# Attention branch product of an encoder layer in seven half-size products instead of eight, with its weights and y kept raw in SBUF

## The chip, the cores and the metric

One core of a Trainium2 chip runs the whole program. A core has five engines with a queue each: TensorE (PE, matrix products out of SBUF into PSUM; PEld is its loading of weights), VectorE (DVE), ScalarE (ACT), GpSimd (POOL) and SyncE (SP, here only a queue that issues DMAs). An engine works its queue in order and waits on semaphores for the others. The metric is device microseconds for one execution, the median of several runs.

## The reference

The program is one layer of an encoder, 1024 positions of 1024 channels in float32:

```python
h = rmsnorm(x, g_mix)
z = h @ w_in                                   # pooling channels | q | k | v
y_pool = pool_mixer(u_pool, w_pool_grp, pool_scale)          # S x 512
y_attn = diff_attention(q, k, v, g_q, g_k, lam, g_sub, ...)  # S x 1024, 8 heads
gates = sigmoid(h @ w_gate + b_gate)                         # S x 2048
merged = (gates[..., :D] * (y_pool @ w_branch_pool)
          + gates[..., D:] * (y_attn @ w_branch_attn))
x = x + merged @ w_out
h2 = rmsnorm(x, g_ffn)
x = x + square(relu(h2 @ w_up)) @ w_down
```

The change lies in `merged`: the product with `w_branch_attn` (1024 x 1024 by 1024 x 1024, transposed: channels in partitions, positions along the row) and the gating of both branches.

## The kernel before

**Precision.** Each product is made of three: an operand is split into a high part, rounded to fp32r by a cast on ACT (`split`, L120), and a low part, operand minus high part, on DVE or POOL (L121). `mm3` (L126 to L128) adds hi x hi, hi x lo and lo x hi in one PSUM bank. So each operand tile costs one ACT cast and one subtraction, and each 128 x 128 x 512 block three matmuls.

**Stages.** Attention with the products for the gates and the pooling mixer as filler ends at about 701 us of the span. `g_dram` then holds the gates before their sigmoid, `y_dram` and `r_dram` the attention output and its row factors, `p_dram` the pooling branch. After it come three stages and then the MLP (up from 926 us, down to the end):

- *bp*, 701 to 745 us: `branch_pool` makes 16 tiles of 128 channels by 512 positions, 12 matmuls each (four blocks of depth 128), out of `wbp` and `ypT`. ACT copies each tile from PSUM to `mp`. Beside it `y_scaled` loads y and multiplies it with its factors (`ry`, L215), and `split_halves` makes `yT` of it, high and low part for all 8 blocks of depth; both stay in SBUF for the next stage.
- *ba*, 745 to 832 us: for each block d of 128 channels `load_cols` loads and splits one column block of the weights (`wba`, low part on POOL), `gate` loads the gates and takes their sigmoid, DVE multiplies `mp` with its gate (L837). Then two tiles of 24 matmuls; each is multiplied with its gate out of PSUM (`mg`, L844, DVE), POOL adds `mp` (L845), and `split` makes `mT`, the operand of the next stage (cast on ACT, low part on DVE).
- *op*, 832 to 926 us: `out_proj` multiplies `mT` with w_out (`wo`, low part on POOL), adds x and norms the rows.

**Order of the work.** The kernel is written as a program in one order; a scheduler then sets the order of each engine's queue by its own estimate of when operands and buffers are there, and puts in the semaphores. Buffers rotate in pools: a load or a write into a slot waits until the last reader of what lay there has finished. PSUM has eight banks, and `bank` takes them in turn.

Of the kernel before, what the change touches and what calls it, by code (L numbers as in the profile page):

```python
# [32 lines left out]
N_U, N_W, N_RAW, N_V = 11, 8, 2, 6  # L33
# [2 lines left out]
N_Z, N_S, N_T, N_F = 2, 2, 2, 1  # L36
N_YU = 5
N_QKVW = 8 * H
ROOMS = "WWFFWWWFFWWW"
N_AHEAD_Y = 4  # L40


START = "x0 g n0 w0 w1 w2u w3u x1 s0p s1 x2 s2p s3 x3"
# [14 lines left out]
def encoder_kernel(  # L58
# [32 lines left out]
    hp1 = mix.enter_context(tc.tile_pool(name="hp1", bufs=8))  # L91
# [9 lines left out]
    hcount = [0]  # L101

    def htile(shape, dt, name, th):

        if th == 0:
            hcount[0] += 1
        return (hp1 if th else hp0[(hcount[0] - 1) // 4 % 2]).tile(shape, dt, tag="H", name=name)
# [10 lines left out]
    def split(hi, lo, src, lo_eng=None):  # L118

        nc.scalar.copy(hi, src)  # L120
        (lo_eng or nc.vector).tensor_tensor(lo, src, f(hi), op=ALU.subtract)  # L121

    def mm3(ps, lhs_hi, lhs_lo, rhs_hi, rhs_lo, first, last, more=False):

        kw = {"skip_group_check": True} if more else {}
        nc.tensor.matmul(ps, lhs_hi, rhs_hi, start=first, stop=False, **kw)  # L126
        nc.tensor.matmul(ps, lhs_hi, rhs_lo, start=False, stop=False, **kw)  # L127
        nc.tensor.matmul(ps, lhs_lo, rhs_hi, start=False, stop=last, **kw)  # L128

    wcount = [0]  # L130

    def wt(shape, name):

        wcount[0] += 1
        if wcount[0] > N_QKVW and ROOMS[(wcount[0] - N_QKVW - 1) // 2] == "F":
            return fw_tile(shape, name)
# [14 lines left out]
    def load_cols(src, c0, name, nk=NK):

        rw = raw([P, nk, P], f"r{name}")
        nc.sync.dma_start(rw, src[0 : nk * P, c0 : c0 + P].rearrange("(kk p) c -> p kk c", p=P))
        ws = []
        for j in range(0, nk, 4):
            w = wt([P, 2, 4, P], f"w{name}_{j}")
            split(w[:, 0], w[:, 1], rw[:, j : j + 4, :], nc.gpsimd)
            ws.append(w)
        return ws  # L160

    def load_cols2(src, c0, name):

        rw = raw([P, 4, 2 * P], f"r{name}")
        nc.sync.dma_start(rw, src[0 : 4 * P, c0 : c0 + 2 * P].rearrange("(kk p) c -> p kk c", p=P))
        ws = []
        for j in range(2):
            w = wt([P, 2, 4, P], f"w{name}_{j}")
# [49 lines left out]
    def gate(gts, c):  # L218
        for gt, c0, c1 in gts:
            nc.sync.dma_start(gt, g_dram[c * P : (c + 1) * P, c0:c1])  # L220
            nc.scalar.activation(gt, gt, AF.Sigmoid, bias=zero)

    def whole(g):
        return [(g, 0, S)], [g[:, 0:512], g[:, 512:S]]
# [12 lines left out]

# [565 lines left out]
    nbank.append(0)  # L803


    def row_factors(d):
        if d < N_AHEAD_Y or d == 5:
            return [fu_tile(f"rb{d}")]
        if d == 4:
            return [ut([P, S], F32, f"rb{d}")]  # L810
        return [tmp(f"rb{d}_{i}") for i in range(2)]

    ws_bp = {0: load_cols2(w_branch_pool, 0, "bp0")}
    ys = {d: y_scaled(d, row_factors(d)) for d in range(N_AHEAD_Y)}
    ypT = [load_split(p_dram, g * P, f"ypT{g}", ypt_tile) for g in range(4)]
    mp, yT, ws_ba = [], [], {}

    for d in range(NK):
        if d % 2 == 0 and d + 2 < NK:
            ws_bp[d + 2] = load_cols2(w_branch_pool, (d + 2) * P, f"bp{d + 2}")  # L820
        elif d > NK - 4:
            j = len(ws_ba)
            ws_ba[j] = load_cols(w_branch_attn, j * P, f"ba{j}")
        branch_pool(d, ws_bp[d - d % 2][d % 2], bank)
        yT.append(split_halves(ys.pop(d), f"yT{d}", yt_tile(d)))
        if d + N_AHEAD_Y < NK:
            ys[d + N_AHEAD_Y] = y_scaled(d + N_AHEAD_Y, row_factors(d + N_AHEAD_Y))
    mT = {}
    for d in range(NK):
        if d + 3 < NK:  # L830
            ws_ba[d + 3] = load_cols(w_branch_attn, (d + 3) * P, f"ba{d + 3}")
        ws = ws_ba.pop(d)
        gp = [tmp(f"gp{d}_{th}") for th in range(2)]
        gate([(gp[0], 0, 512), (gp[1], 512, S)], d)
        for th in range(2):
            mh = mp[d][:, th * 512 : (th + 1) * 512]
            nc.vector.tensor_tensor(mh, mh, gp[th], op=ALU.mult)  # L837
        ga = fu_tile(f"ga{d}") if d % 2 else ut([P, S], F32, f"ga{d}")
        gate(whole(ga)[0], NK + d)
        for th in range(2):  # L840
            hs = slice(th * 512, (th + 1) * 512)
            ps = proj_T(bank(f"ba{d}_{th}"), ws, lambda k, th: pair(yT[k][th]), th)
            mg = tmp(f"mg{d}_{th}")
            nc.vector.tensor_tensor(mg, ps, ga[:, hs], op=ALU.mult)  # L844
            nc.gpsimd.tensor_tensor(mg, mg, mp[d][:, hs], op=ALU.add)  # L845
            t = htile([P, 2, 512], F32R, f"mT{d}_{th}", th)
            split(t[:, 0, :], t[:, 1, :], mg)
            mT[d, th] = t
# [365 lines left out]
    b11 = {}  # L1218
# [117 lines left out]
```

## Time and profile before

| what | value |
|---|---|
| median of 3 runs | 1549.02 us (1548.29 to 1549.4) |
| the profiled execution | 1548.34 us, its span 1546.6 us |
| granted TensorE clock | 1.0 |
| TensorE busy | 1526.0 us, 99% of the span |
| stage bp | 701.3 to 745 us |
| stage ba | 745 to 832 us |
| stage op | 832 to 926 us |

All durations are from the one profiled execution. A row of a group reads: line, engine, operation, output <- inputs by their names in the program, shape, count | busy time, mean ns of one | idle time of the engine ahead of them and who ended it. A row of the timeline reads: start us, length us, engine, line, operation, and in brackets how long the engine sat idle before it. In the table by stretches of time each engine has its busy time and, in parentheses, its count of instructions; then the granted clock and the DMA engines' share. Since matmuls overlap in the pipeline, the length of one (390 ns for 512 columns) is not the interval between two.

### The profile page before, as it was taken

To read this page: it belongs to the slowest core of one execution; us is meant where nothing else is said; L and a number is where in the kernel's file an instruction comes from. 1 tells how busy PE (TensorE), PEld (TensorE's weight loads), DVE (VectorE), ACT (ScalarE), POOL (GpSimd) and SP (SyncE) were. 2 spreads that over 40 slices of the span, in tenths; PEclk is the share of its full clock that TensorE was granted. 3 is DMA by queue.
4 is the path that set the end of the run, shared out by engine and by line. 5 is a ranking of instruction groups with operands and counts; after the bars stand their busy time and mean duration, and the time that the engine had idled before them with its cause. 6 is when DMAs were issued, how large, how long until landed. Compare 5 with 4: busy or idle time off the path is not lost.

```text
span 1546.6 us, 22053 instructions
## 1 busy us (share of the span) xinstructions
PE 1526.0 (99%) x7649; PEld 1320.4 (85%) x7649; DVE 1012.4 (65%) x2268; ACT 816.5 (53%) x1808; POOL 350.9 (23%) x448
## 2 busy tenths in 40 slices
PE   7999999999999999999999999999999999999999
PEld 6899999999998989888888887888888788888887
DVE  7777777777878787865322448766666668556672
ACT  6656555666666565566432546565555634333331
POOL 6433334243525262315443400000000000000000
PEclk9999999999999999999999999999999999999999
DMA  7111212020202031547426534555432789537650
GB/s 230 49 54 48 64 39 73 20 79 32 81 28 84 28 96 42 177 132 250 139 93 205 177 105 124 180 172 176 137 136 109 259 312 389 196 123 256 225 192 28
DMA packets 166681, 206.41 MB, mean 133 GB/s; under 512 B 10069, under 2 KB 102954, under 8 KB 166570
## 3 DMA queue, kind: packets, MB, share of 16 engines
q1 hardware_dynamic: 149162, 177.71, 34.8%
q10 hardware_dynamic: 17408, 27.30, 4.7%
q8 instruction: 60, 0.98, 0.3%
q14 instruction: 51, 0.42, 0.1%
HBM read 150.42 MB, written 54.56 MB: 133 GB/s over the span
## 4 chain that ended last, share of the span: by engine, by line
PE 91%; DVE 3%; issue 2%; ACT 1%; DMA 1%; POOL 1%; SPq 1%; POOLq 0%; DVEq 0%; ACTq 0%
PE z L126 5%; PE z L128 5%; PE z L127 5%; PE Da L126 4%; PE Da L127 4%; PE Da L128 4%; PE g L126 3%; PE g L127 3%; PE g L128 3%; PE Db L126 3%; PE Db L127 3%; PE Db L128 3%; PE X L126 2%; PE X L128 2%; PE X L127 2%; PE sc L512 2%
## 5 line engine op out<-in xcount | busy, mean ns | idle before, releaser
L126 PE MATMUL z<-wqkv,hT 128*128 128x384 f32 x512 | 174.5, 341 | 0.4 <-DVE qn L453 0.3
L128 PE MATMUL z<-wqkv,hT 128*128 128x384 f32 x512 | 174.1, 340 | 0.0
L127 PE MATMUL z<-wqkv,hT 128*128 128x384 f32 x512 | 173.8, 339 | 0.0
L522 ACT ACTIVATE s<-s,nm 128x256 f32<-128x256 f32 (+7 forms) x128 | 99.6, 778 | 45.8 <-DVE nm L514 42.7
L260 POOL TENSOR_TENSOR ms<-ms,mhalf 128x4 f32<-128x4 f32 x64 | 66.5, 1039 | 158.0 <-DVE ms L259 136.7
L126 PE MATMUL g<-hT,fwgate 128*128 128x512 f32 x256 | 101.0, 395 | 0.1
L127 PE MATMUL g<-hT,fwgate 128*128 128x512 f32 x256 | 101.0, 395 | 0.0
L128 PE MATMUL g<-hT,fwgate 128*128 128x512 f32 x256 | 101.0, 395 | 0.0
L126 PEld LDWEIGHTS z<-wqkv,hT 128*128 128x128 f32 x512 | 96.8, 189 | 3.9 <-DVE qn L453 1.0
L127 PEld LDWEIGHTS z<-wqkv,hT 128*128 128x128 f32 x512 | 96.6, 189 | 3.0
L128 PEld LDWEIGHTS z<-wqkv,hT 128*128 128x128 f32 x512 | 96.6, 189 | 2.2 <-DVE hT L121 0.5
L514 DVE CUSTOM_DVE_ANT_0 s<-sc,dist 128x512 f32<-128x512 f32 (+3 forms) x128 | 74.7, 586 | 19.7 <-PE sc L512 18.2
L121 POOL TENSOR_TENSOR wqkv<-rqkv,wqkv 128x384 fp32r<-128x384 f32 x60 | 64.0, 1085 | 19.2 <-ACT wqkv L120 15.5
L121 DVE TENSOR_TENSOR AS<-s,AS 128x512 fp32r<-128x512 f32 x64 | 43.9, 688 | 35.8 <-ACT AS L120 35.6
L511 PE MATMUL sc<-K,Q 128*128 128x512 f32 (+2 forms) x192 | 66.6, 353 | 0.1
L512 PE MATMUL sc<-K,Q 128*128 128x512 f32 (+2 forms) x192 | 66.5, 354 | 0.0
L459 POOL TENSOR_TENSOR qn<-qn,ggh 128x128 f32<-128x128 f32 x64 | 32.3, 505 | 138.7 <-DVE qn L453 127.7
L485 ACT CAST Q<-tk 64x128 fp32r<-64x128 f32 x128 | 33.2, 259 | 57.8 <-DVE Q L484 56.0
L482 ACT CAST Q<-tk 64x128 fp32r<-64x128 f32 x128 | 33.0, 258 | 53.7 <-DVE K L481 52.3
L121 POOL TENSOR_TENSOR fwgate<-frgate,fwgate 128x512 fp32r<-128x512 f32 x32 | 44.5, 1394 | 51.9 <-ACT fwgate L120 51.8
L128 PEld LDWEIGHTS g<-hT,fwgate 128*128 128x128 f32 x256 | 48.1, 188 | 8.6
L126 PEld LDWEIGHTS g<-hT,fwgate 128*128 128x128 f32 x256 | 48.2, 188 | 7.3 <-ACT go L757 0.4
(430 smaller groups left out, 4640.7 us busy)
## 6 DMA issues: line engine op xcount, KB each, us to landing
wd<-in_w_down_dram SPq DMA_DIRECT2D x56, 512.0 KB, 5.3
wu<-in_w_up_dram SPq DMA_DIRECT2D x32, 512.0 KB, 4.5
udS<-us SPq DMA_DIRECT2D x64, 256.0 KB, 2.4
ur<-udS SPq DMA_DIRECT2D x32, 512.0 KB, 3.3
rqkv<-in_w_in_dram SPq DMA_DIRECT2D x64, 192.0 KB, 2.7
ud<-u ACTq DMA_DIRECT2D x48, 256.0 KB, 2.1
ur<-ud SPq DMA_DIRECT2D x24, 512.0 KB, 4.7
frgate<-in_w_gate_dram SPq DMA_DIRECT2D x32, 256.0 KB, 2.6
```

What stands on the lines that cost most here:

```text
L121: (lo_eng or nc.vector).tensor_tensor(lo, src, f(hi), op=ALU.subtract)
L126: nc.tensor.matmul(ps, lhs_hi, rhs_hi, start=first, stop=False, **kw)
L127: nc.tensor.matmul(ps, lhs_hi, rhs_lo, start=False, stop=False, **kw)
L128: nc.tensor.matmul(ps, lhs_lo, rhs_hi, start=False, stop=last, **kw)
L260: nc.gpsimd.tensor_tensor(dst, dst, mhalf[:, :n], op=ALU.pow)
L459: nc.gpsimd.tensor_tensor(qn[:, 2:4, :], qn[:, 2:4, :], ggh.unsqueeze(1).broadcast_to([P, 2, HD]), op=ALU.mult)
L482: nc.scalar.copy(q_hi, q)
L485: nc.scalar.copy(Q[other, m, 1, :], q)
L511: nc.tensor.matmul(dst, Q[:, i, 0, :], rhs, start=True, stop=False)
L512: nc.tensor.matmul(dst, Q[:, i, 1, :], rhs, start=False, stop=True)
L514: nc.vector.tensor_tensor_reduce(out=s[i][:, c : c + w], in0=sc[:, 0:w], in1=dist[:, o0 + c : o0 + c + w], scale=2.0 ** -(h + 1), scalar=B ...
L522: nc.scalar.activation(s[i][:, 0:n], s[i][:, 0:n], AF.Exp, bias=last, scale=-1.0, accum_out=Z[:, i, t : t + 1])
```

## The change

The product with `w_branch_attn` is cut into quarters of 512 x 512 x 512: weights a11, a12, a21, a22 and y b11, b12, b21, b22. Instead of eight products of quarters it makes seven, over sums and differences of quarters, in the order 1, 2, 6, 7, 5, 4, 3 (Winograd's form of Strassen's product). Four products of the seven go on adding to a bank that holds another's result, and copies of three partial results are kept in SBUF ("slabs" x1, U2, z7). Each product has four steps of depth 128, and a step is 12 matmuls, over four banks.

- Raw weights come in contiguous rows (`load_wr`, 8 x 512 KB) and stay in SBUF as `wr`, as y does in `ry`; the sums overwrite them in place on DVE (`first_sums`, `second_sums`, `third_sums`: 32 operations of 128 x 512).
- Three steps ahead of TensorE, `prepare` splits the two operands of a step: `wa` (cast ACT, low part POOL) into one of four "fw" slots and `yb` (cast ACT, low part DVE) into one of four "B" slots. `wba` and `yT` go, with their splits: 16 of each before, 28 of each now.
- `after` takes a product's banks: 12 copies on ACT, 12 additions from PSUM on DVE ("plus"). `gated` multiplies with the gate on DVE and adds `mp` on POOL, 16 times; 12 of the multiplies now read a slab in SBUF where all 16 of `mg` read PSUM. `merged` makes `mT` as before.
- In bp each tile is multiplied with its gate as it leaves PSUM (DVE); the copy on ACT goes.
- All gates are loaded in halves of 512 columns, in four rotating slots (`gate_half`).

```diff
+    def load_wr(k):
+        wr[k] = ut([P, S], F32, f"wr{k}")
+        nc.sync.dma_start(wr[k], w_branch_attn[k * P : (k + 1) * P, :])
...
     def branch_pool(d, ws, ps_fn):
         m = htile([P, S], F32, f"mp{d}", 1)
+        gs_ = [gate_half(d, th) for th in range(2)]
         for th in range(2):
             ps = proj_T(ps_fn(f"bp{d}_{th}"), ws, lambda k, th: pair(ypT[k][th]), th, nk=4)
-            nc.scalar.copy(m[:, th * 512 : (th + 1) * 512], ps)
+            nc.vector.tensor_tensor(m[:, th * 512 : (th + 1) * 512], ps, gs_[th], op=ALU.mult)
...
+    def gate_half(r0, th):
+        gt = tmp(f"g{r0}_{th}")
+        nc.sync.dma_start(gt, g_dram[r0 * P : (r0 + 1) * P, th * 512 : (th + 1) * 512])
+        nc.scalar.activation(gt, gt, AF.Sigmoid, bias=zero)
+        return gt
...
+    def second_sums(kk):
+        a11, a12, a21, a22, b11, b12, b21, b22 = raws_of(kk)
+        s2, t2 = sums[kk]
+        nc.vector.tensor_tensor(s2, a22, a21, op=ALU.subtract)
+        nc.vector.tensor_tensor(t2, b12, b11, op=ALU.add)
+    def third_sums(kk):
+        a11, a12, a21, a22, b11, b12, b21, b22 = raws_of(kk)
+        s2, t2 = sums[kk]
+        nc.vector.tensor_tensor(a11, s2, a11, op=ALU.add)
+        nc.vector.tensor_tensor(b11, b22, t2, op=ALU.subtract)
+        nc.vector.tensor_tensor(a12, a12, s2, op=ALU.subtract)
+        nc.vector.tensor_tensor(b21, b21, t2, op=ALU.subtract)
...
+    def prepare(j, kk):
+        a11, a12, a21, a22, b11, b12, b21, b22 = raws_of(kk)
+        if j == "6":
+            t = (up_slab, e_slab, e_slab, mx_slab)[kk](f"st2_{kk}")
+            sums[kk] = t[:, 0, :], t[:, 1, :]
+            second_sums(kk)
+            a, b = sums[kk]
+        else:
+            a, b = {
+                "1": (a11, b11), "2": (a12, b21), "5": (a11, b11), "7": (a21, b12), "4": (a22, b21), "3": (a12, b22),
+            }[j]
+        wa = fw_tile([P, 2, 512], f"wa{j}_{kk}")
+        split(wa[:, 0, :], wa[:, 1, :], a, nc.gpsimd)
+        yb = vpool.tile([P, 2, 512], F32R, tag="B", name=f"yb{j}_{kk}", bufs=4)
+        split(yb[:, 0, :], yb[:, 1, :], b)
+        if j == "7":
+            third_sums(kk)
+        ops_ba[j, kk] = wa, yb
+    def ba_step(banks, j, kk):
+        wa, yb = ops_ba.pop((j, kk))
+        acc = j in "6543"
+        for dd in range(4):
+            c = slice(dd * P, (dd + 1) * P)
+            mm3(
+                banks[dd], wa[:, 0, c], wa[:, 1, c], yb[:, 0, :], yb[:, 1, :],
+                not acc and kk == 0, kk == 3, acc,
+            )
+    def gated(d, th, c, src=None):
+        nc.vector.tensor_tensor(c, src or c, gate_half(NK + d, th), op=ALU.mult)
+        nc.gpsimd.tensor_tensor(c, c, mp[d][:, th * 512 : (th + 1) * 512], op=ALU.add)
...
+    def plus(name, banks):
+        for c, ps in zip(kept_ba[name], banks):
+            nc.vector.tensor_tensor(c, ps, c, op=ALU.add)
+        return list(enumerate(kept_ba[name]))
+    def after(j):
+        if j == "1":
+            copies("x1", Xb, [h_slab(f"x1_{i}") for i in range(2)])
+        elif j == "2":
+            for dd, c in plus("x1", Yb):
+                gated(dd, 0, c)
+                merged(dd, 0, c)
+        elif j == "6":
+            copies("U2", Xb, [up_slab(f"bU2_{i}") for i in range(2)])
+        elif j == "7":
+            copies("z7", Yb, [h_slab(f"z7_{i}") for i in range(2)])
+        elif j == "5":
+            for dd, c in plus("z7", Xb):
+                gated(4 + dd, 1, c)
+        elif j == "4":
+            for dd, c in plus("U2", Yb):
+                gated(4 + dd, 0, c)
+                merged(4 + dd, 1, kept_ba["z7"][dd])
+                merged(4 + dd, 0, c)
+        else:
+            for dd, c in enumerate(slabs([e_slab(f"c12_{i}") for i in range(2)])):
+                gated(dd, 1, c, Xb[dd])
+                merged(dd, 1, c)
+    for n, (j, kk) in enumerate(order):
+        if n + N_AHEAD_B < len(order):
+            prepare(*order[n + N_AHEAD_B])
+        ba_step(Xb if j in "1653" else Yb, j, kk)
+        if kk == 3:
+            after(j)
```

The queues move most where ba hands over to op. POOL's queue there, before: the additions of `mp` and the low parts of `wo`, two and two.

```order
L845 TENSOR_TENSOR mg5_1_9509<-mg5_1_9509,mp5_8916 128x512
L845 TENSOR_TENSOR mg6_0_9551<-mg6_0_9551,mp6_8959 128x512
L121 TENSOR_TENSOR wo11_4_0_9842<-ro11_4_9840,wo11_4_0_9842 128x512
L121 TENSOR_TENSOR wo11_4_1_9845<-ro11_4_9840,wo11_4_1_9845 128x512
L845 TENSOR_TENSOR mg6_1_9582<-mg6_1_9582,mp6_8959 128x512
L845 TENSOR_TENSOR mg7_0_9624<-mg7_0_9624,mp7_9002 128x512
```

And in the changed kernel, from the first addition of U2 on (`bU2`; `wa3_3` is the weight of the last ba step, `c12` the result of product 3):

```order
L871 TENSOR_TENSOR bU2_0_9351<-bU2_0_9351,mp4_8887 128x512
L119 TENSOR_TENSOR wa3_3_9655<-wr7_9045,wa3_3_9655 128x512
L871 TENSOR_TENSOR bU2_0_9351<-bU2_0_9351,mp5_8924 128x512
L871 TENSOR_TENSOR bU2_1_9352<-bU2_1_9352,mp6_8967 128x512
L871 TENSOR_TENSOR bU2_1_9352<-bU2_1_9352,mp7_9010 128x512
L119 TENSOR_TENSOR wo00_4_0_9792<-ro00_4_9790,wo00_4_0_9792 128x512
L119 TENSOR_TENSOR wo00_4_1_9795<-ro00_4_9790,wo00_4_1_9795 128x512
L871 TENSOR_TENSOR c12_0_9709<-c12_0_9709,mp0_8707 128x512
L119 TENSOR_TENSOR wo00_6_0_9800<-ro00_6_9798,wo00_6_0_9800 128x512
L871 TENSOR_TENSOR c12_0_9709<-c12_0_9709,mp1_8744 128x512
L119 TENSOR_TENSOR wo00_6_1_9803<-ro00_6_9798,wo00_6_1_9803 128x512
```

The additions for three quarters of the channels now stand in one run with the last weights of ba and with half of the `wo` that the first output tile reads; before, that tile's `wo` had been split earlier and the second set was under way.

DVE at the same place, in the changed kernel: the last `yb`, two gates of U2, then `mT` with the gates of product 3 (out of `baX`) between them. `mT7_0`, the last row, is the last operand of the first output tile. Before, this place has one `mg` and one `mT` in turn.

```order
L119 TENSOR_TENSOR mT4_0_9619<-bU2_0_9351,mT4_0_9619 128x512
L119 TENSOR_TENSOR mT5_1_9627<-z7_0_9433,mT5_1_9627 128x512
L119 TENSOR_TENSOR mT5_0_9630<-bU2_0_9351,mT5_0_9630 128x512
L119 TENSOR_TENSOR mT6_1_9638<-z7_1_9434,mT6_1_9638 128x512
L870 TENSOR_TENSOR c12_0_9709<-baX0_9065,g8_1_9711 128x512
L119 TENSOR_TENSOR mT6_0_9641<-bU2_1_9352,mT6_0_9641 128x512
L870 TENSOR_TENSOR c12_0_9709<-baX1_9066,g9_1_9719 128x512
L119 TENSOR_TENSOR mT7_1_9649<-z7_1_9434,mT7_1_9649 128x512
L870 TENSOR_TENSOR c12_1_9710<-baX2_9067,g10_1_9727 128x512
L870 TENSOR_TENSOR c12_1_9710<-baX3_9068,g11_1_9735 128x512
L119 TENSOR_TENSOR mT0_1_9716<-c12_0_9709,mT0_1_9716 128x512
L119 TENSOR_TENSOR mT7_0_9652<-bU2_1_9352,mT7_0_9652 128x512
```

Eight of the sixteen `mT` now stand here, behind all other work of ba; before they were spread over the stage, one per tile.

ACT at the same place, in the changed kernel: sigmoids of gates (L774, each behind its load) and casts.

```order
L774 ACTIVATE g10_1_9727<-g10_1_9727,zero_124 128x512
L118 CAST mT6_1_9638<-z7_1_9434 128x512
L774 ACTIVATE g11_1_9735<-g11_1_9735,zero_124 128x512
L118 CAST mT6_0_9641<-bU2_1_9352 128x512
L118 CAST mT7_1_9649<-z7_1_9434 128x512
L118 CAST wo00_6_0_9800<-ro00_6_9798 128x512
L118 CAST wo00_6_1_9803<-ro00_6_9798 128x512
L118 CAST mT0_1_9716<-c12_0_9709 128x512
L118 CAST mT7_0_9652<-bU2_1_9352 128x512
```

A cast of `mT` or `wo` waits here behind a gate's load; before, one sigmoid of a whole gate (128 x 1024) stood between every four casts.

More of the change, by code (lines that the diff above doesn't have):

```diff
@@ L38 @@
 N_QKVW = 8 * H
-ROOMS = "WWFFWWWFFWWW"
-N_AHEAD_Y = 4
+N_AHEAD_B = 3
 START = "x0 g n0 w0 w1 w2u w3u x1 s0p s1 x2 s2p s3 x3"
@@ L90, in encoder_kernel @@
     hp0 = [mix.enter_context(tc.tile_pool(name=f"hp0{i}", bufs=4)) for i in "ab"]
-    hp1 = mix.enter_context(tc.tile_pool(name="hp1", bufs=8))
+    hp1 = [mix.enter_context(tc.tile_pool(name=f"hp1{i}", bufs=4)) for i in "ab"]
     wpool = mix.enter_context(tc.tile_pool(name="wpool", bufs=1))
@@ L99, in encoder_kernel @@
     ps_f = mix.enter_context(tc.tile_pool(name="ps_f", bufs=N_F, space=PSUM))
-    hcount = [0]
+    hcount = [0, 0]
     def htile(shape, dt, name, th):
-        if th == 0:
-            hcount[0] += 1
-        return (hp1 if th else hp0[(hcount[0] - 1) // 4 % 2]).tile(shape, dt, tag="H", name=name)
+        hcount[th] += 1
+        return (hp1 if th else hp0)[(hcount[th] - 1) // 4 % 2].tile(shape, dt, tag="H", name=name)
     def ut(shape, dt, name):
@@ L128, in mm3 @@
         nc.tensor.matmul(ps, lhs_lo, rhs_hi, start=False, stop=last, **kw)
-    wcount = [0]
     def wt(shape, name):
-        wcount[0] += 1
-        if wcount[0] > N_QKVW and ROOMS[(wcount[0] - N_QKVW - 1) // 2] == "F":
-            return fw_tile(shape, name)
         return wpool.tile(shape, F32R, tag="W", name=name, bufs=N_W)
@@ L149, in fu_tile, with load_cols2 @@
         return fq.tile([P, S], F32, tag="fu", name=name)
[L151 to L162, printed above, removed]
+    def load_cols2(src, c0, name, tile_fn):
         rw = raw([P, 4, 2 * P], f"r{name}")
@@ L167, in load_cols2 @@
         for j in range(2):
-            w = wt([P, 2, 4, P], f"w{name}_{j}")
+            w = tile_fn([P, 2, 4, P], f"w{name}_{j}")
             split(w[:, 0], w[:, 1], rw[:, :, j * P : (j + 1) * P], nc.gpsimd)
@@ L216, in y_scaled @@
         return rw
[L218 to L224, printed above, removed]
     def pair(t):
@@ L775, in encoder_kernel @@
         pass
-    vpool = attn.enter_context(tc.tile_pool(name="vpool", bufs=N_V))
+    vpool = attn.enter_context(tc.tile_pool(name="vpool", bufs=1))
     pb = mix.enter_context(tc.tile_pool(name="pb", bufs=5, space=PSUM))
-    nbank = [0]
-    def vt(shape, dt, name):
-        return vpool.tile(shape, dt, tag="V", name=name)
+    nbank = [0, 0]
     def bank(name):
@@ L793, in ypt_tile @@
         return htile(shape, dt, name, 0)
-    def yt_tile(d):
-        fn = ut if d < N_YU else vt
-        return lambda shape, dt, name, th: fn(shape, dt, name)
     def tmp(name):
@@ L801, in tmp @@
         return fr_tile([P, 512], name) if nbank[1] % 4 in (1, 2) else fo_tile(name)[:, 0:512]
-    nbank.append(0)
-    def row_factors(d):
[L807 to L814, printed above, removed]
-    ypT = [load_split(p_dram, g * P, f"ypT{g}", ypt_tile) for g in range(4)]
@@ L816, in encoder_kernel @@
-    mp, yT, ws_ba = [], [], {}
+    def gate_half(r0, th):
[3 more added lines that the diff above has]
+        return gt
+    def row_factors(d):
+        return [fu_tile(f"rb{d}")] if d in (0, 1, 2, 3, 5) else [tmp(f"rb{d}_{i}") for i in range(2)]
+    ws_bp = {0: load_cols2(w_branch_pool, 0, "bp0", wt)}
+    yr, wr, mp, mT = {}, {}, [], {}
+    for d in range(NK - 2):
+        yr[d] = y_scaled(d, row_factors(d))
@@ new lines, in encoder_kernel, with quarters, raws_of @@
+    ypT = [load_split(p_dram, g * P, f"ypT{g}", ypt_tile) for g in range(4)]
+    def load_wr(k):
+        wr[k] = ut([P, S], F32, f"wr{k}")
+        nc.sync.dma_start(wr[k], w_branch_attn[k * P : (k + 1) * P, :])
+    def quarters(t, kk):
+        return [t[kk + j][:, i * 512 : (i + 1) * 512] for i, j in ((0, 0), (0, 4), (1, 0), (1, 4))]
+    def raws_of(kk):
+        a11, a12, a21, a22 = quarters(wr, kk)
+        b11, b21, b12, b22 = quarters(yr, kk)
+        return a11, a12, a21, a22, b11, b12, b21, b22
@@ new lines, in first_sums @@
+    def first_sums(kk):
+        a11, a12, a21, a22, b11, b12, b21, b22 = raws_of(kk)
+        nc.vector.tensor_tensor(a21, a11, a21, op=ALU.subtract)
+        nc.vector.tensor_tensor(b12, b22, b12, op=ALU.subtract)
+    def second_sums(kk):
[10 more added lines that the diff above has]
+        nc.vector.tensor_tensor(b21, b21, t2, op=ALU.subtract)
@@ new lines, in slabs, with up_slab, e_slab, mx_slab @@
+    def slabs(tiles):
+        return [t[:, i, :] for t in tiles for i in range(2)]
+    def up_slab(name):
+        return ut([P, 2, 512], F32, name)
+    def e_slab(name):
+        return vpool.tile([P, 2, 512], F32, tag="E", name=name, bufs=2)
+    def mx_slab(name):
+        return fq.tile([P, 2, 512], F32, tag="mx", name=name)
+    def h_slab(name):
+        return hp0[1].tile([P, 2, 512], F32, tag="H", name=name)
+    sums, ops_ba = {}, {}
+    def prepare(j, kk):
+        a11, a12, a21, a22, b11, b12, b21, b22 = raws_of(kk)
+        if j == "6":
[14 more added lines that the diff above has]
+        ops_ba[j, kk] = wa, yb
@@ L818, in encoder_kernel, with merged @@
+    def merged(d, th, c):
+        mT[d, th] = t = (hp1 if th else hp0)[d // 4].tile([P, 2, 512], F32R, tag="H", name=f"mT{d}_{th}")
+        split(t[:, 0, :], t[:, 1, :], c)
+    order = [(j, kk) for j in "1267543" for kk in range(4)]
     for d in range(NK):
         if d % 2 == 0 and d + 2 < NK:
[L820 to L823, printed above, removed]
+            ws_bp[d + 2] = load_cols2(w_branch_pool, (d + 2) * P, f"bp{d + 2}", fw_tile)
@@ L824, in encoder_kernel @@
         branch_pool(d, ws_bp[d - d % 2][d % 2], bank)
[L825 to L848, printed above, removed]
@@ new lines, in encoder_kernel, with copies @@
+        if d == 1:
+            for k in (6, 7):
+                yr[k] = y_scaled(k, row_factors(k))
+        load_wr(d)
+        if d > 4:
+            prepare(*order[d - 5])
+    for kk in range(4):
+        first_sums(kk)
+    Yb = [bank(f"baY{dd}") for dd in range(4)]
+    Xb = [bank(f"baX{dd}") for dd in range(4)]
+    kept_ba = {}
+    def copies(name, banks, tiles):
+        kept_ba[name] = slabs(tiles)
+        for c, ps in zip(kept_ba[name], banks):
+            nc.scalar.copy(c, ps)
@@ new lines, in plus @@
+    def plus(name, banks):
+        for c, ps in zip(kept_ba[name], banks):
+            nc.vector.tensor_tensor(c, ps, c, op=ALU.add)
[23 more added lines that the diff above has]
+                merged(dd, 1, c)
```

## The prediction

> **What bounds the kernel now.** I read the head of the page first, then the busy table by stage, then the list of what TensorE waited for.
>
> ```profile
> span 1546.6 us, 22053 instructions
> PE 1526.0 (99%) x7649; PEld 1320.4 (85%) x7649; DVE 1012.4 (65%) x2268; ACT 816.5 (53%) x1808; POOL 350.9 (23%) x448
> ...
> core 0: us, PE busy (x) PEld busy (x) DVE busy (x) ACT busy (x) POOL busy (x), PEclk, DMA share, GB/s
> 701.30:745.00 43.70, 43.70 (x195) 36.05 (x193) 21.62 (x30) 28.59 (x48) 18.59 (x14) 1.00 0.64 209
> 745.00:832.00 87.00, 87.00 (x385) 72.09 (x384) 24.30 (x34) 31.03 (x47) 44.11 (x34) 1.00 0.34 109
> 832.00:926.00 94.00, 94.00 (x444) 78.06 (x444) 37.40 (x63) 39.11 (x75) 21.50 (x21) 1.00 0.53 176
> ...
> PE hps L286 <- DVE hn L281: 9.6, 2, 8.9
> PE X L126 <- ACT U L1094: 1.6, 1, 1.6
> ```
>
> TensorE is busy 99% of the span. The three rows by stage are the pooling branch (bp), the attention branch (ba) and the output projection (op): in each it is busy for the whole stretch, at granted clock 1.00, and none of its waits lies there (the longest by far is at the program's start). So a matmul taken away is time taken away, as long as its operands keep coming. Two more rows date the ba stage and its products.
>
> ```profile
> 745.00 0.39 PE L128 MATMUL bp<-ypT,wbp 128*128 128x512 f32 x1
> 745.22 0.39 PE L126 MATMUL ba<-yT,wba 128*128 128x512 f32 x1
> L126 PE MATMUL ba<-yT,wba 128*128 128x512 f32 x128 | 49.8, 389 | 0.0
> ```
>
> The first ba matmul starts at 745.22; I call that T and count from it. 385 matmuls in 87.00 us are 0.226 us each (the 389 ns of one overlap the next).
>
> **What goes.** ba falls from 384 matmuls (3 x 128) to 336: seven products of 48 instead of eight. 48 x 0.226 = **-10.8 us**. No other matmul comes or goes. Everything else is work for DVE, ACT, POOL and the queues, and costs nothing only while it stays ahead of TensorE, which now leaves ba at T+75.9 instead of T+86.8.
>
> **The pooling branch.** 16 ACT copies out of PSUM go, and the 16 DVE multiplies stay but read PSUM. What is new is that a bank is released only after a gate's load, its sigmoid and that multiply:
>
> ```profile
> gp<-g_dram SPq DMA_DIRECT2D x16, 256.0 KB, 3.6
> ...
> L220 SPq DMA_DIRECT2D ga<-g_dram x8: 319/320/454, 702.3 to 811.4; - x8
> DMA to landing us min/median/max: 3.2/3.2/7.9
> ...
> L221 ACT ACTIVATE gp<-gp,zero 128x512 f32<-128x512 f32 x16 | 11.5, 723 | 11.3 <-DMA gp<-g_dram 11.2
> L844 DVE TENSOR_TENSOR mg<-ba,ga 128x512 f32<-128x512 f32 x16 | 11.0, 689 | 14.5 <-PE ba L128 14.5
> ```
>
> 3.6 + 0.72 + 0.69 = 5.0 us. The gates share four slots, and a bp tile takes 12 x 0.226 = 2.7 us, so a slot comes round every 10.8 us: covered. What can leak is the start: on ACT's queue sigmoids waiting for loads now stand ahead of casts for the last attention head and ahead of the yb casts of the first ba steps, while eight 512 KB weight loads meet a stage whose DMA share is already 0.64. Below it costs nothing; above, a gate load as late as the slowest ga load before (7.9 us, 4.3 over 3.6) is a bound. I take 1 us, because each queue here has some microseconds between need and readiness.
>
> **Instruction load in ba.** Two casts in a row on ACT:
>
> ```profile
> 829.18 0.62 ACT L120 CAST mT<-mg 128x512 fp32r<-128x512 f32 x1 [3.71 <-POOL mg L845]
> 829.74 0.62 ACT L120 CAST wo<-ro 128x512 fp32r<-128x512 f32 x1
> ```
>
> Between T and T+75.9 DVE issues 77 operations (34 before, in the longer stage); at the 0.69 us of mg that is 53 us: it fits. ACT has about 100 at 0.56 us, one start to the next, some of them sigmoids of 0.72: some 60, it fits. POOL has 46 up to the first output tile, against 34; at 1.29 us (wba and mg, below) 59: it fits. Each engine alone has room.
>
> **The row that speaks against the change.** These are DVE's and POOL's rows where both subtract from SBUF:
>
> ```profile
> 717.35 1.28 DVE L121 TENSOR_TENSOR yT<-ry,yT 128x512 fp32r<-128x512 f32 x2
> 719.60 1.31 POOL L121 TENSOR_TENSOR wba<-rba,wba 128x512 fp32r<-128x512 f32 x1 [2.71 <-ACT wba L120]
> 719.67 1.79 DVE L121 TENSOR_TENSOR yT<-ry,yT 128x512 fp32r<-128x512 f32 x1
> 722.19 3.39 POOL L121 TENSOR_TENSOR wba<-rba,wba 128x512 fp32r<-128x512 f32 x2 [1.28 <-ACT wba L120]
> 722.64 1.78 DVE L121 TENSOR_TENSOR yT<-ry,yT 128x512 fp32r<-128x512 f32 x1
> 724.35 1.78 DVE L837 TENSOR_TENSOR mp<-mp,gp 128x512 f32<-128x512 f32 x1
> 726.05 0.68 DVE L121 TENSOR_TENSOR yT<-ry,yT 128x512 fp32r<-128x512 f32 x1
> ...
> 748.94 5.94 POOL L121 TENSOR_TENSOR wba<-rba,wba 128x512 fp32r<-128x512 f32 x4 [5.30 <-ACT wba L120]
> 751.04 2.69 DVE L837 TENSOR_TENSOR mp<-mp,gp 128x512 f32<-128x512 f32 x2 [4.52 <-ACT gp L221]
> ...
> L844 DVE TENSOR_TENSOR mg<-ba,ga x16: 684/691/692, 757.1 to 832.5; 128x512 f32<-128x512 f32 x16
> L121 DVE TENSOR_TENSOR yT<-ry,yT x16: 678/682/1790, 673.3 to 726.1; 128x512 fp32r<-128x512 f32 x16
> L845 POOL TENSOR_TENSOR mg<-mg,mp x16: 1276/1286/1295, 757.9 to 834.4; 128x512 f32<-128x512 f32 x16
> ```
>
> Two yT in a row take 1.28 us, so 0.60 to 0.68 each; beside a POOL subtraction one takes 1.78. They don't overlap, they alternate: from 722.64 to 724.35 to 726.05 one pair takes 1.71 us, 0.60 for DVE and **1.11 for POOL**. The stretch at 748.94 says the same: (5.94 - 2 x 0.60) / 4 = **1.18**. mg, whose one input is in PSUM, never stretches (684 to 692 ns). So what counts is a DVE operation with two SBUF inputs beside any POOL one. I call that joint resource the port.
>
> [...]
>
> Before, ba asked little of the port: wba and yT were made once, mostly ahead, and mT met POOL seldom. Now every product splits its operands anew. Up to mT7_0, the last operand of the first output tile, POOL has 24 wa, 14 adds and 8 wo = 46 operations, and DVE has 24 yb, 8 sums, 12 gates from SBUF and 13 mT = 57. 46 x 1.11 + 57 x 0.60 = 85 us, from T+2.7 on (a wa slot is free after the first step). That ends at T+88 if the port never rests.
>
> TensorE asks for mT7_0's low half after 336 + 38 matmuls: 374 x 0.226 = T+84.5. So the port is **late at the start of op**. Step by step from the end of the fifth product, 240 x 0.226 = T+54.2, which releases the gates of z7: first POOL has 10 operations (wa4_3, four adds of z7, four wa3, one add of U2) and DVE 11 (yb4_3, four gates, four yb3, two gates of U2) before the last ba step is ready: 10 x 1.11 + 11 x 0.60 = 17.7, T+71.9, due at 324 x 0.226 = T+73.2. That just holds. Behind it stand 9 of POOL and 11 of DVE up to mT7_0: 16.6 more, T+88.5, **4.0 us late**. At 1.18 for POOL it is 1.4 more. I take **5**.
>
> The products before are near balance too: after product 2 (T+21.7), 9 of POOL and 13 of DVE (gates, adds, mT, wa7, yb7) take 17.8 and are due by T+40.7 with the sigmoids of the next gates ahead of the casts; 1.2 us of room. Bounds: nothing, and the 4.3 us of a late gate load less that room, 3.1. I take 1.
>
> **The rest.** Less cover for wo: its loads and casts come in the same order, and op's later tiles find them done, since four tiles of 24 matmuls (21.7 us) stand between. MLP-up and MLP-down keep their work: nothing, at most 1 us either way for rows that the scheduler moved.
>
> **Sum**, on the profiled execution's 1548.34 (span 1546.6 and 1.74 around it): 1548.34 - 10.8 + 1 + 1 + 5 = 1544.5. The median of the runs is 1549.02, 0.7 above; so **1545**.
>
> **Rivals.**
> - *The cover holds* (0.20). The port's holds are shorter where three engines' waits spread them, and the interleaved rows hide the op start. For it: DVE and POOL run 24.3 and 44.1 us of the 87 before. Against: the 85 us of port work in 84.5. It gives 1549.0 - 10.8 + 0.5 = 1538.7.
> - *Gate loads chain with the port* (0.17). A gate's slot is freed by a DVE multiply that itself waits for the port; the next load (3.6) and sigmoid (0.72) stand on ACT ahead of the casts for wa and mT. At the op start the fourth U2 gate, two DVE and one POOL operation after T+71.9, is done by T+74.2; load and sigmoid make T+78.5, and six casts and a subtraction bring mT7_0 to T+78.5 + 6 x 0.56 + 0.69 = T+82.6, 1.9 in time. One load of 7.9 there lets the port rest for 4.3 - 1.9 = 2.4, one after product 2 costs 3.1 where I took 1: 4.5 more, 1549.5, no change. For it: ACT idled 11.2 us on gp loads before. Against: their median.
> - *The port costs full durations* (0.19): **slower**. If its holds don't overlap at all, a POOL operation costs 1.29 and a DVE one 0.69: 46 x 1.29 + 57 x 0.69 = 98.7, T+101.4, 16.9 late at the latest at op's first tile, whichever step shows it. 1549.0 - 10.8 + 1 + 16.9 = 1556. It wins over the saving once the port is 10.8 us late. For it: the 3.39 us of two wba. Against: the pair's 1.71. [...]
> - *Seven products don't save* (0.02): product tiles now change banks every three matmuls instead of every 24. The MLP does so already:
>
> ```profile
> 1000.00:1100.00 100.00, 100.00 (x442) 82.78 (x442) 68.14 (x107) 60.81 (x108) 0.00 (x0) 1.00 0.49 166
> ```
>
>   442 in 100 us are the same 0.226, so I give it little: without the saving the port has 10.8 us more and only the two small terms are left, 1549 + 2 = 1551.
>
> **How the numbers follow.** My forecast (partly given back at op's start) has 0.42, from 1541 to 1549. A measurement of this kernel tells 0.2%, 3.1 us, from no change, so faster ends at 1545.9. Faster: all of the first rival and 0.30 of the forecast, 0.50. Same: 0.12 of the forecast, 0.14 of the gate loads, 0.02: 0.28. Slower: 0.19 and 0.03, 0.22. The range runs from 1538 (cover holds) to 1554 (port nearly full price).
>
> **What would show it.** Right: TensorE's waits name DVE mT or POOL wo, 3 to 8 us together, around the first op tile, and yb, mT and wa have maxima near 1.7 while those with a PSUM input stay at 0.69. The cover held: none of these waits. The chain of gate loads: TensorE waits for ACT casts, and ACT idles on loads of g. Full price: waits in every product from the third on. I am wrong outright if the lost time lies before T, or if ba's matmuls come further apart than 0.226 without a wait.

## The result, and the profile after

The changed kernel takes 1561.1 us (median of 6 runs, 1558.47 to 1562.26) beside 1549.11 us of the kernel before: 1.0076 times as long, interval 1.0063 to 1.0089. It is slower by 12.0 us; 1545 was forecast, with 1554 as the upper end.

The head of the page of the changed kernel (lines are its own: 118 and 119 are the split, 124 to 126 the three matmuls, 1023 the last step of a row's norm, 1026 the transposes of the normed row) and the table by stages, the stretches cut at the first matmul of each stage:

```profile
span 1559.6 us, 22122 instructions
PE 1526.1 (98%) x7601; PEld 1314.0 (84%) x7601; DVE 1081.2 (69%) x2325; ACT 826.9 (53%) x1836; POOL 382.0 (24%) x460
...
703.09:747.77 44.68, 43.95 (x194) 35.97 (x193) 23.55 (x37) 17.12 (x29) 13.63 (x11) 1.00 0.57 182
747.77:828.70 80.93, 78.34 (x337) 62.38 (x336) 68.69 (x64) 48.57 (x88) 63.82 (x40) 1.00 0.19 60
828.70:935.91 107.21, 100.55 (x441) 80.24 (x440) 57.86 (x76) 49.09 (x95) 41.63 (x33) 0.95 0.55 174
```

TensorE issues 48 instructions less than before and is busy for as long. The matmuls went; time in which it waited, and time at a lower clock, came. Stage by stage against the profile before (spans 1559.6 and 1546.6, so 13.0 to explain):

| stage | before | after | difference |
|---|---|---|---|
| up to the first bp matmul | 701.5 | 703.1 | +1.6 |
| bp | 43.7 | 44.7 | +1.0 |
| ba | 87.0 | 80.9 | -6.1, where -10.8 was possible |
| op | 93.4 | 107.2 | +13.8 |
| MLP up, to the first matmul of down | 312.3 | 315.1 | +2.8 |

What TensorE waited for, by the list of waits of the changed kernel:

```profile
PE hb L1026 <- DVE y L1023: 3.9, 4, 1.8
PE op L125 <- POOL wo L119: 2.6, 4, 1.0
PE X L124 <- ACT AS L118: 2.2, 1, 2.2
...
PE baY L125 <- DVE yb L119: 1.5, 2, 1.1
PE po L577 <- ACT oqs L118: 1.1, 1, 1.1
PE baX L126 <- POOL wa L119: 1.1, 2, 0.7
...
PE bp L124 <- DVE mp L209: 0.7, 1, 0.7
```

So op lost more than all else, at two places. Cut finer, op shows both, and a clock that was 1.00 throughout before:

```profile
828.70:843.50 14.80, 12.08 (x40) 8.07 (x39) 14.80 (x14) 7.58 (x14) 12.97 (x9) 0.88 0.51 160
843.50:878.20 34.70, 34.70 (x153) 28.45 (x152) 12.79 (x15) 10.36 (x21) 20.07 (x16) 1.00 0.83 246
878.20:890.00 11.80, 7.86 (x28) 5.71 (x28) 9.46 (x13) 8.82 (x17) 6.40 (x5) 0.71 0.42 139
890.00:935.90 45.90, 45.90 (x223) 38.00 (x223) 20.80 (x36) 22.32 (x44) 2.20 (x4) 1.00 0.38 134
```

In the first 14.8 us, at the first output tiles, TensorE issues 39 matmuls of 512 columns, which take 8.8 at 0.227: 6.0 lost. From 878.2 to 890.0, at the first transposes of normed rows, 11 such matmuls and 16 small ones: 7.5 lost. The other two stretches lose 0.3 together.

At the first place the rows point at the port. DVE and POOL of the changed kernel, where product 7 follows product 6, a row each in turn, and the durations of the groups:

```profile
780.82 1.76 DVE L119 TENSOR_TENSOR yb<-ry,yb 128x512 fp32r<-128x512 f32 x1
782.50 1.77 DVE L119 TENSOR_TENSOR mT<-x,mT 128x512 fp32r<-128x512 f32 x1
784.20 1.78 DVE L119 TENSOR_TENSOR yb<-ry,yb 128x512 fp32r<-128x512 f32 x1
...
780.30 1.73 POOL L119 TENSOR_TENSOR wa<-wr,wa 128x512 fp32r<-128x512 f32 x1
781.99 1.73 POOL L871 TENSOR_TENSOR x<-x,mp 128x512 f32<-128x512 f32 x1
783.68 3.44 POOL L119 TENSOR_TENSOR wa<-wr,wa 128x512 fp32r<-128x512 f32 x2
...
L119 DVE TENSOR_TENSOR yb<-ry,yb x24: 677/1286/1779, 721.0 to 823.1; 128x512 fp32r<-128x512 f32 x24
L119 POOL TENSOR_TENSOR wa<-wr,wa x24: 1287/1739/1808, 738.0 to 824.3; 128x512 fp32r<-128x512 f32 x24
L902 DVE TENSOR_TENSOR z<-baX,z x4: 674/678/678, 804.1 to 808.1; 128x512 f32<-128x512 f32 x4
```

Both engines start a row every 1.70 us, the pair price of the prediction (1.71). The median yb lasts 1.29 us instead of 0.68, the median wa 1.74 instead of 1.29, and additions that read PSUM stay at 0.68.

The second place has another chain behind it. The chain of work of the changed kernel that ends at the late transposes (start, length, what) is this, in order of time:

```profile
839.71 3.45 DVE mT L119 x2
...
856.69 0.70 DVE y L946
857.39 2.12 SPq L988
...
859.60 5.10 DMA ro<-in_w_out_dram
864.78 0.63 ACT wo L118
865.48 2.55 POOL wo L119 x2
868.04 3.59 DMA ro<-in_w_out_dram
871.73 0.63 ACT wo L118
...
873.73 1.30 POOL wo L119
875.05 0.37 SPq L158
875.47 5.81 DMA yd<-y
881.39 1.16 ACT y L1020
...
883.17 1.77 DVE y L1023
885.00 1.12 PE hb L1026 x4
```

A load of w_out waits until POOL has split what lay in its raw slot; the next load waits in the same way; the store of a finished row (`yd`) stands behind these loads on SP's queue; the row's norm waits for that store. The second half of the first set of w_out was split late (POOL was done with it at 842.6), and SP's loads of w_out waited 45.8 us in all for POOL's splits. So a chain of slots and queues carried the delay 40 us further. Ahead of 859.60 the same chain leaves the loads: the first of them stood on SP behind a store (857.39), the store waited for DVE's addition to a finished tile (856.69), and TensorE had worked without a break towards that tile since the late `mT` came at 843.16. In this one profile the late first tiles thus feed the late transposes as well, and the chain alone doesn't tell which of the two sets the delay; the experiments do.

### The profile page after: what moved, and what is told of

It is laid out like the page before. It is cut to its first block, busy times and chain, and to the rows that moved or that the text cites. A ratio compares the mean times of both kernels' runs of the same rounds, so it can differ in the third digit from the quotient of the medians.

```text
span 1559.6 us, 22122 instructions
## 1 busy us (share of the span) xinstructions
PE 1526.1 (98%) x7601; PEld 1314.0 (84%) x7601; DVE 1081.2 (69%) x2325; ACT 826.9 (53%) x1836; POOL 382.0 (24%) x460
## 4 chain that ended last, share of the span: by engine, by line
PE 80%; DVE 8%; DMA 5%; issue 3%; ACT 2%; POOL 1%; SPq 1%; POOLq 0%; ACTq 0%; DVEq 0%
PE z L124 5%; PE z L125 5%; PE z L126 5%; PE Da L126 4%; PE Da L124 4%; PE Da L125 4%; PE g L124 3%; PE g L125 3%; PE g L126 3%; PE Db L126 3%; PE Db L124 3%; PE Db L125 3%; PE X L124 2%; PE X L126 2%; PE X L125 2%
## 5 line engine op out<-in xcount | busy, mean ns | idle before, releaser
L119 DVE TENSOR_TENSOR AS<-s,AS 128x512 fp32r<-128x512 f32 x64 | 43.7, 688 | 37.2 <-ACT AS L118 37.1
```

## Experiments

Each kernel below differs from the changed one (1561.1 us) unless said otherwise.

**The additions of mp on DVE.**

```diff
-        nc.gpsimd.tensor_tensor(c, c, mp[d][:, th * 512 : (th + 1) * 512], op=ALU.add)
+        nc.vector.tensor_tensor(c, c, mp[d][:, th * 512 : (th + 1) * 512], op=ALU.add)
```

> The 16 additions of mp in the attention branch go from POOL to DVE; all else as changed. The changed kernel took 1561.1 us: 12.0 more than before, in spite of 10.8 us of matmuls less. Theory P (the port that DVE and POOL share sets ba and the start of op): up to mT7_0 the port has 32 POOL operations of 1.11 and 71 of DVE of 0.60, 78 us instead of 85, so TensorE's waits for yb, wa and wo in ba and at op's first tile shrink by about 7 us, and with them the time at half clock behind them: 1550 to 1555. Theory A (gate loads and sigmoids that stand on ACT ahead of the casts): DVE is only longer, 1559 to 1565. Theory D (DVE alone is too slow): 16 more operations on DVE, 1565 or more.

1554.6 us (1.0039 of before, 1.0026 to 1.0052). Theory P's range holds it, A's and D's don't. In its profile ba still takes 80.6 us, which P had not expected, with one wait of 2.3 for POOL's wa and 3.0 us of half clock behind it (matmuls 0.43 us apart, 784.15 to 787.14); op falls from 107.2 to 100.2. So DVE has room: 16 operations more on it, and the kernel is 6.5 us faster.

**The low parts of wa on DVE as well.**

```diff
-        split(wa[:, 0, :], wa[:, 1, :], a, nc.gpsimd)
+        split(wa[:, 0, :], wa[:, 1, :], a)
```

> The additions of mp and the low parts of wa all go to DVE; POOL keeps only the low parts of wbp and wo. Theory P: up to mT7_0 the port has 8 operations of POOL at 1.11 and 95 of DVE at 0.60, 66 us instead of 85: the waits in ba and at op's first tile go, wo is split in time, its raw slots come free early and the stores of y no longer stand behind late loads on SP, so the waits of the row transposes go too: 1541 to 1547, faster than before. Theory A: 1557 or more. Theory D: about 110 operations on DVE in ba at 0.69 are 76 us of 76, so DVE becomes the bound: 1558 to 1570.

1551.4 us (1.0015, 1.0003 to 1.0026), 4.4 above the range that P gave. The stage table and the waits of this kernel show what held and what didn't:

```profile
749.42:823.76 74.34, 74.34 (x329) 61.57 (x328) 61.77 (x101) 49.10 (x87) 10.73 (x5) 1.00 0.21 66
...
PE hb L1026 <- DVE y L1023: 3.1, 2, 2.1
```

ba is busy from end to end: DVE issues 101 operations there instead of 64 and is busy for 61.8 us instead of 68.7, 0.61 us an operation on the mean instead of 1.07. That part of P is as it expected. The first output tiles no longer wait either. But the transposes still do, and op takes 101.4: splitting wo on a POOL that is nearly idle was not enough. So a second cause was looked for.

**One gate for all tiles of ba.**

```diff
-        nc.vector.tensor_tensor(c, src or c, gate_half(NK + d, th), op=ALU.mult)
+        if not g_once:
+            g_once.append(gate_half(NK, 0))
+        nc.vector.tensor_tensor(c, src or c, g_once[0], op=ALU.mult)
```

> In the attention branch one half gate is loaded and put through the sigmoid once and used for all 16 multiplies: 15 loads and 15 sigmoids of ba are left out (the gates of the other tiles are not applied). The DVE and POOL operations stay. Theory P: the port's work is unchanged; only the one wait at 816.6 us that lies behind a gate's load goes: 1557 to 1561. Theory A: the 5 us of ba and the 7 us of op's first tile go: 1546 to 1551.

1559.5 us (1.0071, 1.0054 to 1.0088), in P's range and far from A's. ba takes 79.0 us instead of 80.9, and the first output tiles still wait (2.3 us for POOL's wo, 0.6 for mT, 1.6 for ACT's wo). Theory A falls. What the loads and sigmoids of gates are worth stays open: the medians are 1.6 us apart and their runs overlap (1557.9 to 1561.4 beside 1558.5 to 1562.3).

**No low parts of wa.**

```diff
-        split(wa[:, 0, :], wa[:, 1, :], a, nc.gpsimd)
+        nc.scalar.copy(wa[:, 0, :], a)
...
-                banks[dd], wa[:, 0, c], wa[:, 1, c], yb[:, 0, :], yb[:, 1, :],
+                banks[dd], wa[:, 0, c], wa[:, 0, c], yb[:, 0, :], yb[:, 1, :],
```

> The 28 low parts of wa are not computed (each third matmul takes the high part in its place, so TensorE does as much as in the changed kernel; the product lacks that correction). POOL loses 28 operations, DVE nothing. Theory P: the port has 22 of POOL at 1.11 and 57 of DVE at 0.60, 59 us instead of 85: waits in ba and at op's first tile go: 1541 to 1547. Theory A or D: 1557 to 1561, since neither ACT's sigmoids nor DVE's count change.

1552.4 us (1.0023, 1.0014 to 1.0033): again ba as P expected, the whole not.

```profile
749.80:825.96 76.16, 76.16 (x338) 63.08 (x336) 52.08 (x65) 51.41 (x91) 25.87 (x18) 1.00 0.20 65
```

DVE does as many operations as in the changed kernel (65, 64) in 52.1 us instead of 68.7. This is the price of the port, seen from DVE: 0.80 us an operation on the mean instead of 1.07, 16.6 us in all. But op takes 100.8 us: its first tiles still wait 1.4 us for POOL's wo (2.6 in the changed kernel), a later tile 1.6 for ACT's, and the transposes 2.5 (3.9).

**Other rooms for w_out.** In `out_proj`'s set-up each half set of w_out gets a room. wo00_4 to 7 had the four fw slots, which in the changed kernel hold wa until the last ba step is multiplied:

```diff
-    ws = {0: w_out_half(0, 0, (w_room, fw_tile))}
+    ws = {0: w_out_half(0, 0, (w_room, w_room))}
...
-    ws = {1: w_out_half(1, 1, (w_room, w_room)), 0: w_out_half(0, 1, (h_room, fw_tile))}
+    ws = {1: w_out_half(1, 1, (w_room, fw_tile)), 0: w_out_half(0, 1, (h_room, w_room))}
```

> Only the rooms of w_out change: the second half of the first set (wo00_4 to 7) goes into the W slots that y leaves as the last yb are made, instead of the four fw slots that wa keeps until product 3 is multiplied; the second set's first half goes to the fw slots. In the changed kernel wo00_4 to 7 can only be cast after T+67.7 to T+75.9. Theory R (late rooms of wo hold the raw slots, so later loads of w_out, stores of y behind them on SP, and the row transposes are late: 13.8 us of op): op's first waits become DVE mT alone and the wait for y L1023 shrinks; op 107 us to 96 to 101: 1549 to 1555. Theory P alone (the port keeps POOL's wo late, rooms don't matter): 1558 to 1562.

1555.2 us (1.0038, 1.0024 to 1.0052), 0.2 above R's range and 2.8 below the other's. op takes 97.9 us instead of 107.2, and the wait of the transposes is gone from the list, as is POOL's wo:

```profile
PE op L126 <- DVE mT L119: 2.6, 2, 1.4
PE X L124 <- ACT AS L118: 2.2, 1, 2.2
PE baX L126 <- POOL wa L119: 2.0, 4, 0.6
...
PE baY L125 <- DVE yb L119: 1.4, 2, 1.1
```

What stays is the port: ba takes 81.7 us. So the losses have two causes, and each fix alone leaves the other's.

**Both.** The second kernel above with these rooms.

> e2_adds_wa_dve (additions of mp and low parts of wa on DVE; 1551.4 us) with the rooms of e5_rooms. Theories P and R together: ba stays dense at 74 to 76 us, op comes back from 101 us to 94 to 97: 1544 to 1547, faster than before. If R is wrong: 1550 to 1553 as in e2_adds_wa_dve.

1543.7 us: 0.9969 of the kernel before, interval 0.9957 to 0.9980. It is faster than both kernels, and 0.3 us under the range that P and R gave together.

```profile
PE 1517.0 (98%) x7601; PEld 1312.0 (85%) x7601; DVE 1073.2 (70%) x2369; ACT 828.5 (54%) x1836; POOL 310.2 (20%) x416
...
747.76:822.11 74.35, 74.35 (x330) 61.56 (x329) 62.19 (x99) 48.73 (x88) 10.68 (x8) 1.00 0.21 69
822.11:917.90 95.79, 95.77 (x449) 78.92 (x448) 55.33 (x83) 49.65 (x95) 26.93 (x24) 1.00 0.58 193
```

ba and op together take 170.1 us, 10.3 less than before (180.4): nearly all of the 10.8. What the whole falls short of that lies outside: 1.7 us ahead of bp, 0.8 in bp, 1.3 in MLP up. (The profiled execution took 1541.9 us, 1.8 less than the median of its six runs.)

**The pooling branch's half of the change undone**, in that kernel, and **alone in the kernel before**:

```diff
-            nc.vector.tensor_tensor(m[:, th * 512 : (th + 1) * 512], ps, gs_[th], op=ALU.mult)
+            nc.scalar.copy(m[:, th * 512 : (th + 1) * 512], ps)
...
+        for th in range(2):
+            mh = m[:, th * 512 : (th + 1) * 512]
+            nc.vector.tensor_tensor(mh, mh, gate_half(d, th), op=ALU.mult)
```

> As e6_dve_rooms, with the second half of the change undone: bp's tiles leave PSUM by an ACT copy as before, and are multiplied with their gates afterwards out of SBUF on DVE. Theory F (PSUM banks that wait for gate loads cost the 0.7 us wait for DVE mp and delay casts at the front): 1 to 2 us faster than e6_dve_rooms. If gating out of PSUM is free: the same within 1 us, or slower by the 16 copies' share of ACT.

The kernel before with bp gated out of PSUM:

```diff
+        gs_ = [tmp(f"gp{d}_{th}") for th in range(2)]
+        gate([(gs_[0], 0, 512), (gs_[1], 512, S)], d)
...
-            nc.scalar.copy(m[:, th * 512 : (th + 1) * 512], ps)
+            nc.vector.tensor_tensor(m[:, th * 512 : (th + 1) * 512], ps, gs_[th], op=ALU.mult)
```

> The kernel before with only the second half of the change: gates loaded in bp, tiles multiplied as they leave PSUM, no ACT copies; ba's product in eight as before. Theory F: the wait at the start of bp costs 1 to 2 us: 1550 to 1551. If it is free: 1549.

1545.8 us (0.9982, 0.9973 to 0.9992) and 1549.4 us (1.0003, 0.9994 to 1.0013). Undone, the kernel is 2.1 us slower, not faster: the wait of bp for a gate goes, but ba waits 1.2 us for the late copies, and the wait for oqs ahead of bp stays (1.0). Alone, it shows neither wait. Theory F falls: by itself gating out of PSUM is free. What is lost ahead of bp then comes with the other half of the change, which loads eight blocks of weights and makes its first sums there; which of the two does it was not tried.

**Zeros written in place of wa's low parts.**

```diff
-        split(wa[:, 0, :], wa[:, 1, :], a, nc.gpsimd)
+        nc.scalar.copy(wa[:, 0, :], a)
+        nc.gpsimd.memset(f(wa[:, 1, :]), 0.0)
```

> POOL writes zeros into each low part of wa instead of subtracting (the product lacks that correction): 28 POOL operations of the same output size in the same queue, which read nothing from SBUF. If any POOL operation takes the port: yb beside such a row still lasts 1.7 to 1.8 us, at most less often, and the mean of yb stays near 1.2 us. If only POOL operations that read SBUF take it: yb beside them lasts 0.68 us and stretches only beside an addition of mp or a split of wo; its mean falls to 0.7 to 0.9, and ba is dense, 76 to 77 us, as in e4_no_wa_low, where the rows were left out.

1553.6 us (1.0033, 1.0021 to 1.0045); ba takes 76.2. Rows of the two engines at one place:

```profile
783.38 0.53 POOL L851 MEMSET wa<- 128x512 f32 x1 [1.84 <-ACT yb L118]
786.10 0.53 POOL L851 MEMSET wa<- 128x512 f32 x1 [2.19 <-PE baY L126]
...
783.48 0.68 DVE L119 TENSOR_TENSOR yb<-ry,yb 128x512 fp32r<-128x512 f32 x1
786.37 0.69 DVE L119 TENSOR_TENSOR yb<-ry,yb 128x512 fp32r<-128x512 f32 x1 [2.21 <-ACT yb L118]
...
L119 DVE TENSOR_TENSOR yb<-ry,yb 128x512 fp32r<-128x512 f32 x24 | 20.3, 851 | 12.6 <-ACT yb L118 12.6
```

Beside a memset, which only writes, yb keeps its 0.68. The mean falls from 1.23 to 0.85; the rest are rows beside additions and splits of wo. A memset is also shorter than a subtraction (0.53 against 1.29), so the mean alone would not tell the two apart; the single rows do.

**Where the kernels lose.** The lengths of ba and op in the profiles, less what their matmuls and transposes take at the rate of the kernel before (0.227 us for 512 columns, 0.115 for a transpose), are the time lost there, in us:

| kernel | ba | first 60 matmuls of op | rest of op |
|---|---|---|---|
| before | 0.0 | 0.0 | 0.0 |
| changed | 4.8 | 6.0 | 7.7 |
| additions of mp on DVE | 4.4 | 4.3 | 2.5 |
| low parts of wa on DVE as well | 0.0 | 0.0 | 6.1 |
| one gate for all tiles | 2.8 | 8.0 | 1.9 |
| no low parts of wa | 0.0 | 1.9 | 5.4 |
| zeros for low parts of wa | 0.0 | 2.2 | 4.3 |
| other rooms for w_out | 5.5 | 4.5 | 0.0 |
| both fixes | 0.0 | 0.2 | 0.3 |
| both fixes, bp's tiles copied by ACT | 1.8 | 0.0 | 0.0 |

ba loses nothing in just those kernels in which POOL no longer subtracts wa, but for the wait for ACT's copies in the last row. The rest of op loses nothing only with the other rooms, though the first tiles are still late there. With the old rooms it loses 1.9 to 7.7 us, also where the first tiles are in time. The first tiles are in time only with the port relieved; the rooms alone bring 6.0 to 4.5. Each row is one profiled execution, so some us can be chance: with one gate these stages lose 5.8 less than in the changed kernel, where the medians differ by 1.6.

## Why the prediction was wrong

- **-10.8 for the matmuls**: right. Where nothing is late, the 336 take 76.2 us; ba and op of the kernel with both fixes have it back but for 0.5.
- **The port**: the mechanism and its price were right, 1.70 us a pair, PSUM readers untouched (0.68). The size was not. ba lost 4.7 us where 1 was taken, op's first tiles 6.0 where 5 was: 10.7 for 6. The ledger's 85 us suppose a port that never rests from T+2.7 on. The trace has nearly the rows that it counts, 45 of POOL and 59 of DVE with both inputs in SBUF, again 85 us at these prices; but they begin at T+3.8 and take 91.5. mT7_0's low half came at 843.2, T+95.4, against T+88.5 to T+90 in the ledger: 5.5 to 6.9 later. About 1.6 us of the 6.0 are no wait at all: the granted clock was 0.52 for the matmuls from 835.1 to 838.5. One reading was too wide: not "any POOL" operation takes the port. The memset, which only writes, didn't: yb took 0.68 us beside it.
- **The step that failed outright is "The rest"**: "its loads and casts come in the same order, and op's later tiles find them done". They didn't. wo00_4 to 7 live in the fw slots that the change fills with wa up to the last step of ba; the prediction counted the slots of wa and yb and not who takes them next. The loss at the transposes was 7.5 us, at a place which the prediction put at nothing, and it is the largest single part of the 17.2 us between the forecast, 1545, and the sum below. The rooms experiment shows the step: with other slots alone, op loses 4.5 us instead of 13.8, and nothing at the transposes. How large the loss is varies (1.9 to 7.7 with the old rooms): in the changed kernel the late first tiles feed it, and half clock (0.51) from 883.0 to 889.9 makes up some 3 of it.
- **MLP up**, taken as 1 us at most, lost 2.8. A wait for AS (2.2) and half clock behind an old wait (0.53 from 1244.8 to 1248.4, worth 1.6) make it up, less a wait for A (0.8) that is gone. With both fixes the wait for AS stays, the half clock doesn't, and the stage loses 1.3; why AS is late was not tried.
- **The front**, 1 taken, 2.6 measured: 1.1 at the wait for oqs, 0.7 at the first gate, the rest in small pieces. Its reason held in part: casts and loads are late there, but banks that wait for gates are free by themselves, as the kernel before with that half alone shows (1.0003).
- **The rivals.** "Full durations", the slower one, had the right side and 1556 us, by a wrong price: the pair is 1.70, not 1.29 + 0.69 = 1.98. That it came nearest was luck: it put nothing at the transposes, and that loss filled the gap. The chain of gate loads was priced at 4.5 us; without its loads the kernel was 1.6 faster, within the spread of the runs, so its size stays open. "The cover holds" fell: ba and op lose next to nothing only where the port's work is taken away and the rooms are changed.

By the sum: 1549.1 - 10.8 + 2.6 + 4.7 + 13.8 + 2.8 = 1562.2 from one profile, the median of the runs being 1561.1.

## What to carry to other kernels

Before work is split anew on DVE and POOL, add up DVE's operations with two inputs in SBUF (0.60 us each here) and POOL's additions and subtractions out of SBUF (1.11, out of pairs of 1.71) as if they were one engine's, and set the sum against the time of the stage; here moving 44 of POOL's operations to a busier DVE left DVE less busy in ba (61.8 us instead of 68.7). When a change fills slots for longer, look up who takes each slot next, in the following stage too, and what stands behind that load in its queue. An idle time of TensorE costs more than itself when the clock drops behind it, as it did here (1.6 to 3 us more).

## What the runs showed of the hardware

**The clock fell after short waits, though not after each.** In the changed kernel two waits of 1.0 and 0.7 us within 3 us (831.4 to 834.5) were followed by 3.5 us at about half clock (0.52 from 835.1 to 838.5). At the transposes the clock fell at the end of the third of four waits (0.6, 1.0, 1.8 and 0.6) and stayed at half for some 6.8 us (0.51 from 883.0 to 889.9). Elsewhere a wait of 1.1 was followed by none (781.1, clock 1.00). The same two waits in MLP up (1.5 for BT1h, 0.8 for u) came with full clock in the kernel before and with half clock in the second experiment; first the rows of that experiment, then those of the kernel before:

```profile
945.80 0.79 PE L124 MATMUL Y<-B21h,A 128*128 128x512 f32 x1 [0.82 <-DVE u L946]
946.40 0.63 PE L125 MATMUL Y<-B21l,A 128*128 128x512 f32 x1
...
945.80:949.10 3.30, 3.29 (x8) 2.62 (x9) 3.30 (x6) 3.30 (x8) 0.00 (x0) 0.52 0.00 0
```

```profile
946.30 0.50 PE L126 MATMUL Y<-B21h,A 128*128 128x512 f32 x1 [0.83 <-DVE u L863]
946.64 0.40 PE L127 MATMUL Y<-B21l,A 128*128 128x512 f32 x1
...
946.30:949.60 3.30, 3.30 (x14) 2.72 (x15) 3.30 (x6) 3.30 (x8) 0.00 (x0) 1.00 0.00 0
```

Matmuls are 0.43 us apart instead of 0.23, eight in 3.3 us instead of 14. So a wait, or a run of them, cost itself, or itself and some 1.6 to 3 us more for the slow matmuls behind it. Gaps of 0.6 to 1.8 us were enough in the changed kernel, and its slow stretches lasted 3.5, some 6.8 and 3.4 us (the last behind the wait of 1.8 for U, 1244.8 to 1248.2). What decides whether a wait brings one was not shown.
